# Thirteen of 64 pairs of k rows of the down projections by Strassen's algorithm, columns in two halves

## The chip, the cores and the metric

The kernel runs on one core of one Trainium2 chip, as one program in one launch. The metric is the device time of that launch in microseconds (us). The engines are called as the profile calls them: PE does matrix multiplications, PEld is its weight load, DVE is the vector engine, ACT the scalar engine, POOL the general one, SP issues most of the loads. SBUF is the memory in which the engines work, PSUM the banks into which PE accumulates. A "tile" here is a named piece of one of them.

## The reference, cut to what matters

A trunk of two decoder layers on 256 tokens of width 2048, all in float32. Layer 0 has stick-breaking attention, layer 1 differential attention; each is followed by a squared-ReLU MLP, and each half of a layer ends in a residual with a factor and a layer norm.

```python
D_MODEL = 2048; SEQ = 256; DEPTH = 2; D_FF = 4 * D_MODEL
DEEPNORM_ALPHA = (2 * DEPTH) ** 0.25

def squared_relu_mlp(x, w_up, w_down):
    h = jax.nn.relu(x @ w_up)
    return (h * h) @ w_down

for layer in range(DEPTH):
    ...   # h = attention of this layer
    x = layer_norm(DEEPNORM_ALPHA * x + h, ln_g[layer, 0], ln_b[layer, 0])
    x = layer_norm(DEEPNORM_ALPHA * x + squared_relu_mlp(x, mlp_w_up[layer], mlp_w_down[layer]),
                   ln_g[layer, 1], ln_b[layer, 1])
```

The down projection multiplies h*h, 256 x 8192, by `w_down`, 8192 x 2048, once per layer. It is the place of the change.

## The kernel before

**Three products for one.** PE is given values of a type (float32r) that keeps fewer bits than float32. Each operand is therefore split into a part `hi`, written by ACT as a copy into that type, and a part `lo`, the difference, written by DVE (`split`, L56 to L62). A product is made of three matmuls, hi·hi, hi·lo and lo·hi, all added up in one PSUM bank. So each weight that comes in costs ACT one pass and DVE one pass before PE can use it, and L59 and L62 are the lines of nearly all of their work.

**Weights.** `wchunk` (L67) loads 128 x 1024 values (512 KB) into one of four staging tiles `st` by a load on SP's queue, takes a pair of tiles `wh` and `wl` from a ring of seven (`ring`, L64), and splits. A chunk is one k row block (128 rows of the weight matrix) by 1024 columns, or two row blocks by 512.

**PSUM.** There are eight banks of 128 x 512: five under the tag "acc", three under the tag "at" (`acc`, L53). "at" also serves transposes and attention.

**The stages.** Layer 0: queries, keys, values and attention, output projection, MLP; layer 1 the same with its own attention. An MLP (`mlp`, L264) first runs the up projection: sixteen blocks of 512 hidden columns. The first goes by token rows and is transposed (L269 to L275); the others go by column (`by_column`, L175), so that the hidden values come out with the hidden index on the partitions, and `folded` (L194) and L280 add the two halves of a bank, apply the squared ReLU and write `hT`, sixteen tiles that hold all of h*h in float32. The operand of the up projection is `xT` (L79), the transposed and split input, one tile of 16 k blocks.

The down projection (L286 to L325) keeps the whole result, 2 blocks of 128 tokens (t) by 4 blocks of 512 columns (n), in the eight banks `a`. It goes once over the 64 k blocks of the hidden index. For every two of them a tile `hp` (two buffers) takes the split of h (L306); for each k, two chunks bring the 2048 columns, and PE does 2 x 4 x 3 = 24 matmuls of 128 x 512. The last `lag` = 5 k blocks are held back and done output by output, so that `residual` (L125) and `layernorm` (L133) of the first token block run while PE works on the second. For these last chunks `space` (L291) lends buffers of `hT` that are no longer read. `load_gb` brings the gain and bias of the layer norm into other such buffers.

**Order of work.** The kernel states tiles and operations; waits, and the place of each operation in its engine's list, are worked out when the program is built. The planner goes by the written order, but puts an operation that it reckons to be ready ahead of one that isn't. Each engine then runs its list from front to back. A tile with `bufs=n` under one tag may exist n times at once; a further one waits until the oldest has been read for the last time.

## Time and profile before

| | |
|---|---|
| device time, median of 3 runs | 2219.82 us (2218.59 to 2220.05) |
| the profiled execution's own time | 2220.36 us |
| its span | 2218.5 us |
| PE, DVE, ACT busy, share of the span | 99%, 61%, 46% |
| moved by DMA | 417.81 MB, mean 188 GB/s |
| PE clock granted, mean | 0.999 |
| up stage of layer 0, about | 428 to 762.6 us |
| down stage of layer 0, about | 762.6 to 1113 us |
| up and down stage of layer 1, about | 1527 to 1859.8, 1859.8 to 2208 us |

The profile is one execution. Times in it are counted from the span's start. Groups of instructions are by line, engine, operation and tile (out<-in), with the count, the busy time in us and the mean duration of one in ns, then the idle time of the engine just before them and what ended it. A row of the timeline or of the chain starts with its start time and its length; "x2" means that two instructions were merged into the row. A stage row gives its window, its length, then for PE, PEld, DVE, ACT and POOL the busy time and the number of instructions in it, the granted PE clock as a share, the mean busy share of the DMA engines, and GB/s. A wait row names the engine and line that waited, who ended the wait, and the total, the count and the longest. Matmuls are pipelined, so the durations of neighbours overlap; their pitch is the distance of their starts.

### The profile page before, as it was taken

The numbers are of one execution on the slowest core, as the hardware profiler recorded it, in microseconds if no ns is written. First come the engines' busy times: TensorE is split into PE (matmuls) and PEld (weight loads), VectorE is DVE, ScalarE is ACT, GpSimd is POOL, SyncE is SP. The second block draws the span as 40 slices with busy tenths as digits, with TensorE's granted clock in tenths as the row PEclk, the third lists the DMA queues.
The fourth block names the chain that finished last, engine by engine and source line by source line (L and its number), as shares of the span: only waits on it lengthen the run. The fifth ranks groups of instructions, "written<-read, shape, count | busy, mean of one in ns | idle before, by whom it ended". The sixth has DMA issues, their size and how long they took to land.

```text
span 2218.5 us, 29307 instructions
## 1 busy us (share of the span) xinstructions
PE 2201.0 (99%) x11314; PEld 1870.9 (84%) x11314; DVE 1360.0 (61%) x1865; ACT 1025.4 (46%) x1346; POOL 14.4 (1%) x20
## 2 busy tenths in 40 slices
PE   8999999999999999999999999999999999999998
PEld 7888888888888888888888888888888888888886
DVE  5776665755555554555678787667555555555546
ACT  5655553444444444444445555434444444444442
POOL 0000000000000000000000000000000000000000
PEclk9999999999999999999999999999999999999999
DMA  8555557566666666666565555556666666666663
GB/s 267 175 161 171 164 174 232 162 190 190 190 190 190 193 216 202 194 192 192 169 205 162 180 159 183 194 186 190 190 189 191 189 190 199 221 196 192 192 196 115
DMA packets 177149, 417.81 MB, mean 188 GB/s; under 512 B 13137, under 2 KB 13649, under 8 KB 177010
## 3 DMA queue, kind: packets, MB, share of 16 engines
q1 hardware_dynamic: 171056, 405.52, 60.0%
q10 hardware_dynamic: 5954, 10.42, 1.5%
q8 instruction: 88, 1.44, 0.3%
q14 instruction: 51, 0.42, 0.1%
HBM read 413.80 MB, written 2.10 MB: 187 GB/s over the span
## 4 chain that ended last, share of the span: by engine, by line
PE 98%; DVE 1%; DMA 0%; issue 0%; ACT 0%; SPq 0%; POOL 0%; DVEq 0%; POOLq 0%; ACTq 0%
PE acc L151 83%; PE at L151 14%; PE at L93 1%; DMA st<-in_sb_w_qkv_dram 0%; DVE wl L62 0%; DVE xs L144 0%; DVE xs L143 0%; PE at L518 0%; PE at L491 0%; DVE stats L128 0%; DVE xs L127 0%; DVE xT L62 0%; PE at L274 0%; ACT wh L59 0%; DVE on L511 0%
## 5 line engine op out<-in xcount | busy, mean ns | idle before, releaser
L62 DVE TENSOR_TENSOR wl<-st,wh 128x1024 fp32r<-128x1024 f32 x768 | 938.5, 1224 | 785.9 <-ACT wh L59 771.5
L59 ACT ACTIVATE wh<-st 128x1024 fp32r<-128x1024 f32 x768 | 811.8, 1059 | 1038.0 <-PE acc L151 956.0
L151 PE MATMUL acc<-xT,wh 128*128 128x512 f32 x2944 | 1016.8, 395 | 0.3 <-ACT k L59 0.3
L151 PE MATMUL acc<-xT,wl 128*128 128x256 f32 x2944 | 790.4, 279 | 0.0
L151 PEld LDWEIGHTS acc<-xT,wh 128*128 128x128 f32 x2944 | 541.4, 188 | 113.0 <-ACT k L59 1.0
L151 PEld LDWEIGHTS acc<-xT,wl 128*128 128x128 f32 x2944 | 553.7, 188 | 15.8
L151 PE MATMUL acc<-wh,hp 128*128 128x512 f32 x1280 | 414.3, 390 | 0.0
L151 PEld LDWEIGHTS acc<-wh,hp 128*128 128x128 f32 x1280 | 240.3, 188 | 49.6
L151 PE MATMUL at<-wh,hp 128*128 128x512 f32 x768 | 256.2, 390 | 0.0
L151 PE MATMUL acc<-wl,hp 128*128 128x512 f32 x640 | 249.4, 390 | 0.0
L151 PE MATMUL acc<-wh,xT 128*128 128x512 f32 x640 | 209.4, 396 | 1.2 <-ACT wh L59 1.2
L151 PEld LDWEIGHTS at<-wh,hp 128*128 128x128 f32 x768 | 144.2, 188 | 29.8
L151 PE MATMUL at<-wl,hp 128*128 128x512 f32 x384 | 149.6, 389 | 0.0
L151 PEld LDWEIGHTS acc<-wh,xT 128*128 128x128 f32 x640 | 120.6, 189 | 26.4 <-ACT wh L59 1.6
L151 PEld LDWEIGHTS acc<-wl,hp 128*128 128x128 f32 x640 | 120.2, 188 | 24.9
L151 PE MATMUL acc<-wl,xT 128*128 128x512 f32 x320 | 126.2, 395 | 0.0
L197 ACT ACTIVATE evb<-acc 128x256 f32<-128x256 f32 x184 | 69.2, 377 | 39.6 <-PE acc L151 35.9
L151 PEld LDWEIGHTS at<-wl,hp 128*128 128x128 f32 x384 | 72.1, 188 | 15.0
L151 PE MATMUL acc<-wh,oTa 128*128 128x512 f32 x256 | 80.5, 391 | 0.0
L151 PE MATMUL acc<-wh,oTb 128*128 128x512 f32 x256 | 80.4, 392 | 0.0
L151 PEld LDWEIGHTS acc<-wl,xT 128*128 128x128 f32 x320 | 60.5, 189 | 11.5
L200 DVE TENSOR_TENSOR evs<-acc,evb 128x256 f32<-128x256 f32 x152 | 60.2, 417 | 0.8
(104 smaller groups left out, 1055.4 us busy)
## 6 DMA issues: line engine op xcount, KB each, us to landing
st<-in_mlp_w_up_dram SPq DMA_DIRECT2D x256, 512.0 KB, 3.7
st<-in_mlp_w_down_dram SPq DMA_DIRECT2D x256, 512.0 KB, 4.2
st<-in_sb_w_qkv_dram SPq DMA_DIRECT2D x96, 512.0 KB, 4.0
st<-in_kv_w_dram SPq DMA_DIRECT2D x64, 512.0 KB, 4.3
st<-in_sb_w_o_dram SPq DMA_DIRECT2D x32, 512.0 KB, 3.9
st<-in_diff_w_q_dram SPq DMA_DIRECT2D x32, 512.0 KB, 4.2
st<-in_diff_w_o_dram SPq DMA_DIRECT2D x32, 512.0 KB, 4.5
gb<-in_ln_g_dram ACTq DMA_DIRECT2D x16, 256.0 KB, 5.1
```

The costliest lines, as they stand in the source:

```text
L59: nc.scalar.activation(hi, src, AF.Copy)
L62: nc.vector.tensor_tensor(lo, src, hi.bitcast(F32), op=ALU.subtract)
L93: nc.tensor.transpose(pt[:, i * P:(i + 1) * P], src[:, i * P:(i + 1) * P], ident)
L151: nc.tensor.matmul(o, l, r, start=start, stop=stop)
L197: nc.scalar.activation(b, psum[:, T:], AF.Copy, scale=scale)
L200: nc.vector.tensor_tensor(s, psum[:, :T], b, op=ALU.add)
```

## The change

The 2048 output columns are done in two halves of 1024, one after the other, each over all 64 k blocks. In a half the result takes four banks (`main`, 2 token blocks by 2 column blocks); the other four are free for `side`. Two k blocks by 1024 columns are called a pair here; there are 32 per half, 64 per layer. A pair is a product of 2 x 2 blocks (token block by k block) with 2 x 2 blocks (k block by column block), eight block products, or 24 matmuls. In 13 of the 64, those numbered 3, 7, ... 27 in the first half and 3, 7, ... 23 in the second, `seven` does it with seven block products (Strassen's algorithm in Winograd's form): sums of hidden blocks (`sf`) and of weight blocks (`t13`, `t24`) are made in float32 on DVE, then split like anything else, and three products go straight into `main`, while p1, p5, p6 and p7 collect in the `side` banks over all sevens of a half. After the last of them `share_out` adds the side banks into the residual `xs`, with the factor ALPHA, and `rest` later adds the main banks.

Further edits: `xT` becomes four tiles under one tag with four buffers, which serve `seven` for sums and their splits between the up projection and the next use of xT; h is split twice, once per half; `hp` has three buffers; the rows held back at the end are the last ten of the second half, in chunks of two row blocks by 512 columns, and `space` lends three pairs of buffers, not four.

The diff, without the lines in which `xT[:, k, ...]` becomes `xT[k // 4][:, k % 4, ...]`:

```diff
+SEVEN = ((3, 7, 11, 15, 19, 23, 27), (3, 7, 11, 15, 19, 23))
...
-    xT = base.tile([P, KT, 2, T], F32R, name="xT")
+    def xtile(name="xT", dtype=F32R):
+        return base.tile([P, 4, 2, T], dtype, tag="xT", bufs=4, name=nm(name))
+
+    xT = [xtile() for _ in range(4)]
...
-            a = [[acc("at"), acc("at"), acc("at"), acc()], [acc() for _ in range(4)]]
-            lag = 5
-            spare = [4]
+            lag = 10
+            spare = [3]
...
-            sets = [[k] for k in range(FT - lag)] + [list(range(FT - lag, FT))]
-            hp = {}
-            for ks in sets:
...
+            def hidden(k, tag="hp", bufs=3):
+                h = pool.tile([P, 2, 2, T], F32R, tag=tag, bufs=bufs, name=nm("hp"))
+                split(h[:, 0], h[:, 1], hT[k // 4][:, k % 4:k % 4 + 2, :])
+                return h
+
+            def three(o, x, w, start, stop):
+                mm(o, x[0], w[0], start, False)
+                mm(o, x[0], w[1], False, False)
+                mm(o, x[1], w[0], False, stop)
+
+            def seven(k, n0, main, side, first, end):
+                st = [wp.tile([P, 2, 512], F32, tag="st", bufs=ST_BUFS, name=nm("st")) for _ in range(2)]
+                for kk in range(2):
+                    nc.sync.dma_start(st[kk], down[(k + kk) * P:(k + kk + 1) * P, n0:n0 + CH].rearrange(
+                        "p (a b) -> p a b", a=2))
+                (b11, b12), (b21, b22) = [[s[:, a, :] for a in range(2)] for s in st]
+                tf, sx, tw13, tw24 = [xtile(n, d).rearrange("p a c t -> p (a c t)") for n, d in (
+                    ("tf", F32), ("sp", F32R), ("tw", F32R), ("tw", F32R))]
+                t13, t24 = [tf[:, i * CH:(i + 1) * CH].rearrange("p (a b) -> p a b", a=2) for i in range(2)]
+                sf = pool.tile([P, 4, P], F32, tag="r", bufs=2, name=nm("sf"))
+                sp = sx[:, :CH].rearrange("p (c a b) -> p c a b", c=2, a=4)
+                tw13, tw24 = [(w[:, :CH], w[:, CH:]) for w in (tw13, tw24)]
+                h = hidden(k)
+                hf = hT[k // 4][:, k % 4:k % 4 + 2, :]
+                a11, a21, a12, a22 = [hf[:, i // 2, i % 2 * P:(i % 2 + 1) * P] for i in range(4)]
+                tt = nc.vector.tensor_tensor
+                w11 = ring()
+                split(w11[0][:, :512], w11[1][:, :512], b11)
+                w2 = ring()
+                split(w2[0], w2[1], st[1].rearrange("p a b -> p (a b)"))
+                tt(sf[:, 0, :], a21, a22, op=ALU.add)
+                tt(sf[:, 1, :], sf[:, 0, :], a11, op=ALU.subtract)
+                tt(sf[:, 2, :], a11, a21, op=ALU.subtract)
+                tt(sf[:, 3, :], a12, sf[:, 1, :], op=ALU.subtract)
+                split(sp[:, 0], sp[:, 1], sf)
+                tt(t13[:, 0, :], b12, b11, op=ALU.subtract)
+                tt(t13[:, 1, :], b22, b12, op=ALU.subtract)
+                tt(t24[:, 0, :], b22, t13[:, 0, :], op=ALU.subtract)
+                tt(t24[:, 1, :], b21, t24[:, 0, :], op=ALU.subtract)
+                split(*tw13, tf[:, :CH])
+                split(*tw24, tf[:, CH:])
...
+                p1, p5, p6, p7 = side
+                three(p1, x(0, 0), cols(w11, 0), first, end)
+                three(main[0][0], x(1, 0), cols(w2, 0), False, False)
+                three(main[0][1], xsum(3), cols(w2, 1), False, False)
+                three(p5, xsum(0), cols(tw13, 0), first, end)
+                three(p7, xsum(2), cols(tw13, 1), first, end)
+                three(p6, xsum(1), cols(tw24, 0), first, end)
+                three(main[1][0], x(1, 1), cols(tw24, 1), False, False)
+
+            def share_out(side, nh):
+                p1, p5, p6, p7 = side
+                y = [[xs[:, t, (2 * nh + n) * 512:(2 * nh + n + 1) * 512] for n in range(2)] for t in range(NT)]
+                u, v = [pool.tile([P, 512], F32, tag="r", bufs=2, name=nm("r")) for _ in range(2)]
+                stt, tt = nc.vector.scalar_tensor_tensor, nc.vector.tensor_tensor
+                nc.scalar.activation(u, p1, AF.Copy)
+                stt(y[0][0], y[0][0], ALPHA, p1, op0=ALU.mult, op1=ALU.add)
+                stt(y[0][1], y[0][1], ALPHA, p5, op0=ALU.mult, op1=ALU.add)
+                stt(y[1][1], y[1][1], ALPHA, p5, op0=ALU.mult, op1=ALU.add)
+                tt(u, u, p6, op=ALU.add)
+                tt(v, u, p7, op=ALU.add)
+                tt(y[0][1], y[0][1], u, op=ALU.add)
+                stt(y[1][0], y[1][0], ALPHA, v, op0=ALU.mult, op1=ALU.add)
+                tt(y[1][1], y[1][1], v, op=ALU.add)
+
+            def rest(t, n, psum):
+                y = xs[:, t, n * 512:(n + 1) * 512]
+                nc.vector.tensor_tensor(y, y, psum, op=ALU.add)
+                nc.vector.bn_stats(stats[t][:, n, :], y)
+
+            fast = SEVEN
+            side = [acc() for _ in range(4)]
+            main = [[acc("at"), acc("at")], [acc("at"), acc()]]
+            for nh in range(2):
+                n0 = nh * CH
+                if nh == 1:
+                    main, old = [[acc() for _ in range(2)] for _ in range(NT)], main
+                    for t in range(NT):
+                        for n in range(2):
+                            rest(t, n, old[t][n])
+                    side = [acc("at"), acc("at"), acc("at"), acc()]
+                for j in range(FT // 2 - (lag // 2 if nh else 0)):
+                    k = 2 * j
+                    if nh == 1 and k == FT // 2:
+                        gb = load_gb(layer, 1, gb_of, hT[k // 4][:, 0, 0:1])
+                    if j in fast[nh]:
+                        seven(k, n0, main, side, j == fast[nh][0], j == fast[nh][-1])
+                        if j == fast[nh][-1]:
+                            share_out(side, nh)
+                        continue
+                    h = hidden(k)
+                    for kk in range(2):
+                        wh, wl = wchunk(down[(k + kk) * P:(k + kk + 1) * P, n0:n0 + CH].rearrange(
+                            "(a p) n -> p a n", p=P))
...
+            ks = list(range(FT - lag, FT))
+            hs, chunks = {}, {}
+            for i, k in enumerate(ks[::2]):
+                hs[k] = hidden(k) if i < 3 else hidden(k, "hT", FT // 4)
+            for n in range(2):
+                for k in ks[::2]:
+                    chunks[k, n] = wchunk(down[k * P:(k + 2) * P, n0 + n * 512:n0 + (n + 1) * 512].rearrange(
+                        "(a p) n -> p a n", p=P), space if n == 1 and k >= FT - 6 else ring)
+            if not last:
+                xT[:] = [xtile() for _ in range(4)]
+            for t in range(NT):
+                for n in range(2):
+                    for k in ks:
...
+                    rest(t, 2 + n, main[t][n])
+                layernorm(t, stats[t], gb, last)
```

More of the change, by code (lines that the diff above doesn't have):

```diff
@@ L296, in space @@
                 return [pool.tile([P, CH], F32R, tag="hT", bufs=FT // 4, name=nm(s)) for s in ("wh", "wl")]
-            sets = [[k] for k in range(FT - lag)] + [list(range(FT - lag, FT))]
-            hp = {}
-            for ks in sets:
-                chunks = {}
-                for k in ks:
-                    if k % 2 == 0:
-                        tag, bufs = ("hT", FT // 4) if k == FT - 2 else ("hp", 2)
-                        hp[k // 2] = pool.tile([P, 2, 2, T], F32R, tag=tag, bufs=bufs, name=nm("hp"))
-                        split(hp[k // 2][:, 0], hp[k // 2][:, 1], hT[k // 4][:, k % 4:k % 4 + 2, :])
-                        if k == FT // 2:
-                            gb = load_gb(layer, 1, gb_of, hT[k // 4][:, 0, 0:1])
-                    for nh in range(2):
-                        chunks[k, nh] = wchunk(
-                            down[k * P:(k + 1) * P, nh * CH:(nh + 1) * CH].rearrange("(a p) n -> p a n", p=P),
-                            space if len(ks) > 1 and nh else ring)
-                for t in range(NT):
-                    ts = slice(t * P, (t + 1) * P)
-                    for n in range(4):
-                        ns = slice(n % 2 * 512, (n % 2 + 1) * 512)
-                        for k in ks:
-                            h, (wh, wl) = hp[k // 2], chunks[k, n // 2]
-                            mm(a[t][n], h[:, 0, k % 2, ts], wh[:, 0, ns], k == 0, False)
-                            mm(a[t][n], h[:, 0, k % 2, ts], wl[:, 0, ns], False, False)
-                            mm(a[t][n], h[:, 1, k % 2, ts], wh[:, 0, ns], False, k == FT - 1)
-                        if ks[-1] == FT - 1:
-                            residual(t, n, a[t][n], stats[t])
-                    if ks[-1] == FT - 1:
-                        layernorm(t, stats[t], gb, last)
@@ new lines, in hidden, with x, xsum, cols @@
+            def hidden(k, tag="hp", bufs=3):
[37 more added lines that the diff above has]
+                split(*tw24, tf[:, CH:])
+                def x(kk, t):
+                    return [h[:, c, kk, t * P:(t + 1) * P] for c in range(2)]
+                def xsum(i):
+                    return [sp[:, c, i, :] for c in range(2)]
+                def cols(w, a):
+                    return [p[:, a * 512:(a + 1) * 512] for p in w]
+                p1, p5, p6, p7 = side
[6 more added lines that the diff above has]
+                three(main[1][0], x(1, 1), cols(tw24, 1), False, False)
@@ new lines, in rest @@
+            def rest(t, n, psum):
[28 more added lines that the diff above has]
+                            for n in range(2):
+                                ns = slice(n * 512, (n + 1) * 512)
+                                three(main[t][n], [h[:, c, kk, t * P:(t + 1) * P] for c in range(2)],
+                                      (wh[:, 0, ns], wl[:, 0, ns]), k + kk == 0, nh == 0 and k + kk == FT - 1)
@@ L328, in trunk @@
+            for t in range(NT):
+                for n in range(2):
+                    for k in ks:
+                        h, (wh, wl) = hs[k - k % 2], chunks[k - k % 2, n]
+                        three(main[t][n], [h[:, c, k % 2, t * P:(t + 1) * P] for c in range(2)],
+                              (wh[:, k % 2, :], wl[:, k % 2, :]), False, k == FT - 1)
+                    rest(t, 2 + n, main[t][n])
+                layernorm(t, stats[t], gb, last)
     with tc.tile_pool(name="sb", bufs=1) as pool:
```

18 lines of the change are left out of this document (9 added, 9 removed).

## The prediction

> **What bounds the kernel now.** First the page's engine shares and the chain that ended last, then the two down stages in the stage table (time, engine busy times, clock, DMA).
>
> ```profile
> span 2218.5 us, 29307 instructions
> PE 2201.0 (99%) x11314; PEld 1870.9 (84%) x11314; DVE 1360.0 (61%) x1865; ACT 1025.4 (46%) x1346; POOL 14.4 (1%) x20
> PE 98%; DVE 1%; DMA 0%; issue 0%; ACT 0%; SPq 0%; POOL 0%; DVEq 0%; POOLq 0%; ACTq 0%
> ...
> 762.60:1111.00 348.40, 348.39 (x1545) 288.39 (x1544) 188.52 (x197) 152.47 (x163) 0.92 (x1) 1.00 0.62 193
> 1859.80:2208.00 348.20, 348.20 (x1537) 288.25 (x1536) 185.13 (x192) 145.29 (x154) 0.92 (x1) 1.00 0.60 189
> ```
>
> The chain lies on PE for 98% of the span. In the down stages PE has no gap at all, at full clock (1.00), while DVE works 188.5 of 348.4 us, ACT 152.5, the DMA engines 62%. A matmul taken away there shortens the kernel by its whole pitch, as long as what the change gives DVE still fits behind PE. The pitch stands in the chain in order of time; one k row of weights shows as 15 matmuls on "acc" banks, with 9 on "at" banks between the rows:
>
> ```profile
> 764.79 3.40 PE acc L151 x15
> 770.23 3.40 PE acc L151 x15
> ...
> 1080.31 3.40 PE acc L151 x15
> ```
>
> From the first to the last are 58 k rows: (1080.31 − 764.79) / 58 = 5.44 us, so 5.44 / 24 = 0.2267 us for each 128x512 matmul, from the first row to the last (3.40 / 15 agrees). 1536 of them make 348.2 us, the length of a down stage.
>
> What waits for whom, over the whole span, says how far ahead of PE the weights are prepared:
>
> ```profile
> ACT wh L59 <- PE acc L151: 956.0, 564, 15.4
> PEld acc L151 <- DVE xT L62: 0.9, 2, 0.4
> PEld acc L151 <- ACT xT L59: 0.8, 3, 0.3
> ```
>
> ACT spends 956 us waiting until PE gives back one of the seven pairs of weight buffers; the waits of PE on prepared data are under 1 us each. Preparation is ahead by the whole ring.
>
> **What is removed.** A pair of k rows by half the columns (a "pair" below) takes 2 k × 2 token blocks × 2 column blocks × 3 = 24 matmuls, 5.44 us. `seven` issues 7 × 3 = 21, 4.76 us. 13 pairs per layer, 2 layers: 78 matmuls fewer, all 128x512 with 128x128 weights as before: 78 × 0.2267 = **−17.68 us**. The bytes read stay: two 512 KB loads per pair.
>
> **What is added on DVE.** Groups by line and shape; the first three rows are from the first down stage alone, the others from the whole span:
>
> ```profile
> L62 DVE TENSOR_TENSOR wl<-st,wh 128x1024 fp32r<-128x1024 f32 x119 | 145.6, 1226 | 151.6 <-ACT wh L59 146.6
> L59 ACT ACTIVATE wh<-st 128x1024 fp32r<-128x1024 f32 x119 | 125.7, 1057 | 166.6 <-PE acc L151 164.8 <-DMA st<-in_mlp_w_down_dram 1.6
> L62 DVE TENSOR_TENSOR hp<-hT,hp 128x512 fp32r<-128x512 f32 x29 | 19.9, 684 | 0.0
> ...
> L59 ACT ACTIVATE hp<-hT 128x512 fp32r<-128x512 f32 x64 | 40.3, 632 | 15.8 <-PE acc L151 15.7
> L127 DVE SCALAR_TENSOR_TENSOR xs<-xs,acc 128x512 f32<-128x512 f32 x26 | 17.4, 683 | 17.9 <-PE acc L151 17.9
> L128 DVE BATCH_NORM_STATS2 stats<-xs 128x6 f32<-128x512 f32 x32 | 21.6, 690 | 0.5
> L143 DVE SCALAR_TENSOR_TENSOR xs<-xs,mv,gb 128x512 f32<-128x512 f32 x32 | 22.7, 746 | 0.0
> L485 DVE SCALAR_TENSOR_TENSOR e<-e,rs,e 128x128 f32<-128x128 f32 x8 | 2.8, 346 | 0.0
> ```
>
> An ordinary pair costs DVE one hp split and two wl splits: 0.684 + 2 × 1.226 = 3.14 us under 5.44 of PE. A seven costs seven ops on 128x512 (hp, w11, sp, four weight sums), three on 128x1024 (w2, tw13, tw24) and four on 128x128 (the hidden sums): 7 × 0.684 + 3 × 1.226 + 4 × 0.346 = 9.85 us, against 4.76 of PE. The sevens stand every fourth pair, so the balance is over four: DVE 9.85 + 3 × 3.14 = 19.26 us, PE 4.76 + 3 × 5.44 = 21.08. DVE fits at 91%, by full durations. Overlap between neighbours takes some off:
>
> ```profile
> 2169.86 2.36 DVE L62 TENSOR_TENSOR wl<-st,wh 128x1024 fp32r<-128x1024 f32 x2 [1.34 <-ACT wh L59]
> ```
>
> Two splits back to back take 2.36, not 2 × 1.226 = 2.45, so some 0.09 per op; over 14 + 9 ops 2.1 us: 17.2, or 81%, is the lower bound. ACT: five more 512-wide or wider passes per seven, 3 × 0.632 + 3 × 1.057 = 5.07 us, with three ordinary pairs of 2.75 us 13.3 of 21.08.
>
> Balance over four pairs is worth nothing without lookahead. Call 0 the time at which PE leaves one seven. The ring holds seven chunks, so by then the three ordinary pairs behind it (16.32 us of PE) can be split already, and the slot for the next w11 is free; w2's comes free 2.72 later, the xT buffers of tf, sp and tw at 0, the hp slot (now three) at 5.44, when the first of the three pairs is done. DVE's 9.85 us can thus be over at 10 to 12, and PE wants them at 16.32: 4 us of slack. Taken as 0; what it costs if the cover is gone is the first rival. The two staging buffers that a seven holds during its sums leave two for the next chunks, and a load lands in 4.2 us against 5.44 per two chunks:
>
> ```profile
> st<-in_mlp_w_down_dram SPq DMA_DIRECT2D x256, 512.0 KB, 4.2
> ```
>
> The second pass over hT repeats 32 hp splits per layer (counted above, one per pair). `share_out` adds 8 DVE ops twice per layer, 8 × 0.683 = 5.5 us, and `rest` does at the half's seam 4 × (0.683 + 0.690) = 5.5 us of what used to be at the end.
>
> **What is moved, and queues.** After the last seven of a half `share_out` waits for p6, and at the seam `rest` waits for the first half's last matmuls; both stand in the code ahead of the next chunks on DVE. Whether those queue behind depends on the order of DVE's list. The same situation exists at the end of the up projections, where `folded` and hT of the last block wait for PE (L200, L280), in the timeline (DVE's rows, and PE's first down matmul):
>
> ```profile
> 761.11 1.22 DVE L62 TENSOR_TENSOR wl<-st,wh 128x1024 fp32r<-128x1024 f32 x1 [1.55 <-ACT wh L59]
> 762.25 0.75 DVE L200 TENSOR_TENSOR evs<-acc,evb 128x256 f32<-128x256 f32 x2
> 762.59 0.39 PE L151 MATMUL at<-wh,hp 128*128 128x512 f32 x1
> 762.91 0.75 DVE L280 SCALAR_TENSOR_TENSOR hT<-evs 128x256 f32<-128x256 f32 x2
> 763.58 0.42 DVE L200 TENSOR_TENSOR evs<-acc,evb 128x256 f32<-128x256 f32 x1
> 764.22 1.23 DVE L62 TENSOR_TENSOR wl<-st,wh 128x1024 fp32r<-128x1024 f32 x1 [0.22 <-ACT wh L59]
> 765.36 0.42 DVE L280 SCALAR_TENSOR_TENSOR hT<-evs 128x256 f32<-128x256 f32 x1
> 765.70 0.42 DVE L200 TENSOR_TENSOR evs<-acc,evb 128x256 f32<-128x256 f32 x1
> ```
>
> A down chunk's split (764.22) was put between the last blocks' ops, though it is written after all of them: the build's planner lets a later op go ahead of one that isn't ready. PE's own list does it too:
>
> ```profile
> 428.47 0.60 PE L274 MATMUL at<-cst,r 128*128 128x128 f32 x4
> 428.82 0.48 PE L151 MATMUL acc<-xT,wh 128*128 128x512 f32 x1
> 429.32 0.66 PE L274 MATMUL at<-cst,r 128*128 128x128 f32 x4
> ```
>
> A matmul of the next block stands between transposes that are written ahead of it. So the seams are costed near nothing, with three places that can show:
>
> - Start of down: `side` is allocated first and takes four acc banks, so main[1][1] gets the one freed last, at the last evs (765.70 + 0.42 = 766.12 above). PE begins down at 762.59 and would want it after 9 matmuls, at 764.6 (before, a[1][3] was wanted after 21, at 767.4). Cost 0 if PE's list is rearranged, 1.5 us if not; times two layers 0 to 3.0. I take 1.0, near the end that the PE rows support.
> - Tail (last ten k rows of the second half): the third hidden pair needs the hp slot that PE releases only at the tail's start; PE wants it after 12 matmuls, 2.72 us, and it takes 0.632 + 0.684 and up to one 1.226 op in the way, 1.3 to 2.5 plus two handovers: 0 to 1.0 per layer, 0 to 2.0 in all, taken as 0.6. Ring and spare hT buffers hold the ten weight chunks, as before.
> - xT becomes four tiles: at most the 0.9 + 0.8 us of the two PEld waits above could go; taken as 0, −1.7 kept for the range.
>
> The end stays as it is, since the last matmul is still followed by one add, one bn_stats and the layer norm:
>
> ```profile
> 2207.78 0.39 PE L151 MATMUL acc<-wh,hp 128*128 128x512 f32 x1
> 2208.21 0.69 DVE L127 SCALAR_TENSOR_TENSOR xs<-xs,acc 128x512 f32<-128x512 f32 x1 [1.98 <-PE acc L151]
> ...
> 2214.00 1.41 DVE L144 SCALAR_TENSOR_TENSOR xs<-xs,rstd,gb 128x512 f32<-128x512 f32 x2
> ```
>
> **Sum.** −17.68 + 1.0 + 0.6 = −16.1 us. The profiled execution took 2220.36 us, its span 2218.5 and 1.9 around it; it stands 0.54 above the median of 2219.82. 2220.36 − 16.1 = 2204.3, less 0.54: **2203.7 us**. Its own range is −17.68 − 1.7 to −17.68 + 5.0, or 2200.4 to 2207.1.
>
> **Rivals.**
>
> 1. DVE becomes the bound, and the kernel slower. Inside a seven, sp, tw13 and tw24 each go DVE, ACT, DVE; if DVE idles through each ACT pass for want of ready work, 0.632 + 2 × 1.057 = 2.75 us are added: 19.26 + 2.75 = 22.0 over four pairs, 0.93 above PE's 21.08. With 26 sevens that is 24 us: −16.1 + 24 = +8, 2228. Below 21.08 it costs nothing; the break-even is at 16.1 / 26 = 0.62 above, 21.7 us; halfway, a loss of 8 us, 2212. For: the sum of DVE in a down stage, 51 × 3.14 + 13 × 9.85 + 4 × 5.5 + 16 × 0.746 for the layer norms = 322 of PE's 1497 × 0.2267 = 339 us, and the 146.6 us for which DVE waited on ACT in the first down stage. Against: those waits end with ACT's own wait for PE (164.8), they are surplus; the planner fills gaps with other chunks; overlap brings the sum down. Chance of the slower part 0.10, of the halfway part 0.08.
>
> 2. DVE's list keeps the written order at `share_out` and `rest`. After p6's end DVE still has 5 ops (3.4 us), then an hp and a wl split (1.9), while PE has only 0.68 of matmuls left and one more that needs no wl: 4.4 us of PE idle, twice a layer; at the seam rest starts 2 us ahead of the end, so 5.5 + 1.9 − 2.0 − 0.2 = 5.2. 14 us a layer, 28 in all: −16.1 + 28 = +12, 2232. Against: the rows at 764.22 and 428.82. [...] Chance 0.04.
>
> 3. PE's pace is set by the weight loads, not by the streaming.
>
> ```profile
> L151 PEld LDWEIGHTS acc<-wh,hp 128*128 128x128 f32 x1280 | 240.3, 188 | 49.6
> ```
>
> Then a matmul taken away is worth a load, 0.188 us: 78 × 0.188 = 14.7 us, and the time is 2203.7 + 3.0 = 2206.7. Against: a pitch of 0.2267 at every one of 58 k rows, with the loads idle in between. Chance 0.03. [...]
>
> That the sevens don't happen at all isn't open: the code issues 21 matmuls for them in every case.
>
> **How the numbers follow.** Forecast 0.75, rival 1 in two parts 0.08 and 0.10, rival 2 0.04, rival 3 0.03. Range: from 2200.4 up to 2213, which takes in the forecast's own range, rival 1 halfway and rival 3 (by the page too), and leaves out some 0.16 plus the forecast's edges. A measurement of this kernel tells 0.2%, 4.4 us, from no change. Faster by more: the forecast, rival 3 and the larger part of rival 1 halfway, 0.83. Slower by more: rival 2 and most of rival 1, 0.12. Between: 0.05.
>
> **What would show it.** Right: PE's matmul count 78 lower; each down stage some 340 us with PE without gaps, stages before unchanged to 1 us; DVE 80 to 95% busy there; ACT still waiting for PE more than for anything else. Rival 1: PE gaps just ahead of each seven, ended by DVE writing tw or sp, DVE at 100%. Rival 2: gaps of some 4 us at two places per layer, after the last seven of a half, and 5 at the seam, with `share_out` and `rest` ahead of wl on DVE. Rival 3: pitch in the sevens off 0.2267. The start-of-down cost: a gap of up to 1.5 us after the ninth down matmul, ended by the last evs. A loss elsewhere, by a planner that orders the whole program otherwise, would make the prediction wrong in a way that no step here covers.

## The result, and the profile after

| | before | after |
|---|---|---|
| device time, median | 2219.94 us (2218.59 to 2220.71, 4 runs) | 2203.70 us (2202.27 to 2204.24, 4 runs) |
| ratio, with its 95% interval | | 0.9926 [0.9909, 0.9944] |
| the profiled execution's own time, its span | 2220.36, 2218.5 us | 2204.09, 2202.3 us |

The change makes the kernel 16.2 us faster, and the time is the predicted one. In the kernel after, the lines have moved: the split is L60 (ACT) and L63 (DVE), the matmul L155, the transposes L97, the hidden sums of a seven L336 to L339, its weight sums L341 to L344, `share_out` L373 to L380, `rest` L384 and L385, the layer norm L139 to L148.

The page of after, the lines that answer to those of before: span, instructions by engine, shares of the chain.

```profile
span 2202.3 us, 29620 instructions
PE 2182.8 (99%) x11236; PEld 1854.9 (84%) x11236; DVE 1560.0 (71%) x2247; ACT 1116.0 (51%) x1492; POOL 14.4 (1%) x20
PE 97%; DVE 1%; DMA 1%; ACT 0%; issue 0%; SPq 0%; POOL 0%; DVEq 0%; ACTq 0%
```

PE has 78 matmuls fewer (11314 to 11236) and is 18.2 us less busy; DVE has 200 us more and is still not the engine on which the chain lies. The stage table of after: the two down stages (the first from its first matmul to the first one behind it; the second from 0.15 us ahead of its first matmul, which starts at 1852.45, to just behind the start of its last, 2191.55), and two groups of four pairs (one seven and three ordinary pairs) in the first of them. Columns as before: window, length, busy time and instructions of PE, PEld, DVE, ACT, POOL, clock, DMA share, GB/s.

```profile
763.39:1104.87 341.48, 341.47 (x1514) 282.50 (x1513) 287.09 (x376) 195.91 (x233) 0.92 (x1) 1.00 0.61 198
1852.30:2191.80 339.50, 339.50 (x1499) 280.89 (x1497) 280.18 (x367) 188.88 (x225) 0.92 (x1) 1.00 0.60 194
824.08:845.16 21.08, 21.08 (x95) 17.45 (x94) 17.88 (x24) 12.70 (x16) 0.00 (x0) 1.00 0.60 198
845.16:866.24 21.08, 21.08 (x95) 17.45 (x94) 16.98 (x20) 12.69 (x16) 0.00 (x0) 1.00 0.63 199
```

PE has no gap in either stage, at full clock. A group takes 21.08 us, 93 matmuls of 0.2267, and DVE is busy 17.9 or 17.0 of it. The two rows differ by four operations (x24, x20): the hidden sums are made some sevens ahead, one set lies in the first of these groups and none in the second. So a group with a set of hidden sums costs DVE 17.9. The first stage with the transposes that lie in it took 350.34 us before (762.59 to 1112.93), so it lost 8.86 us. The second took 347.94 from its first matmul to its last before (1859.84 to 2207.78) and 339.10 after (1852.45 to 2191.55), so it lost 8.84; 39 matmuls by the pitch are 8.84.

The wait table of after over the whole span, the rows with which ACT, then DVE, then PE waited (total, count, longest):

```profile
ACT wh L60 <- PE acc L155: 685.8, 464, 10.3
ACT wh L60 <- DMA st<-in_mlp_w_down_dram: 20.5, 21, 4.1
...
PE at L97 <- DVE xs L148: 1.0, 1, 1.0
```

ACT still waits for PE above all else, 685.8 us where it was 956.0: preparation is ahead of PE, with less to spare. The last row is new in size: PE's transposes wait 1.0 us for the layer norm.

What the operations of a seven cost on DVE, in the groups by form of after, and one hidden sum in its timeline (start, duration):

```profile
L63 DVE TENSOR_TENSOR tw<-tf,tw 128x1024 fp32r<-128x1024 f32 x52 | 63.6, 1223 | 0.0
L341 DVE TENSOR_TENSOR tf<-st 128x512 f32<-128x512 f32 x26 | 17.8, 686 | 2.2 <-DMA st<-in_mlp_w_down_dram 2.2
...
774.33 0.29 DVE L336 TENSOR_TENSOR sf<-hT 128x128 f32<-128x128 f32 x1
```

They cost what the rows of before said, 1.22 and 0.69 (with 0.68 for the splits of 512); the hidden sums are shorter than the 0.346 taken from another operation of that size. With 0.29 for these and 0.09 of overlap per operation, a seven is 7 × 0.685 + 3 × 1.224 + 4 × 0.29 − 14 × 0.09 = 8.37 us, an ordinary pair 3.14 − 0.27 = 2.87, and a group 8.37 + 3 × 2.87 = 16.98. That it equals the second row above is chance, since this group has no hidden sums in it; the row to compare with is 17.88, so the overlap was not 0.09 but some 0.05 per operation. By this sum an ordinary pair leaves DVE 5.44 − 2.87 = 2.57 us to spare, and a seven takes 8.37 − 4.76 = 3.6 us more than PE gives it. These two numbers return in the experiments; they are estimates, on the low side for DVE's work, by 0.9 us per group.

**The three places where the prediction had put seams.** First the start of down. The timeline of after, PE's first and tenth down matmul, and on DVE the last evs:

```profile
763.39 0.39 PE L155 MATMUL at<-wh,hp 128*128 128x512 f32 x1
764.91 0.75 DVE L204 TENSOR_TENSOR evs<-acc,evb 128x256 f32<-128x256 f32 x2
765.44 0.39 PE L155 MATMUL acc<-wh,hp 128*128 128x512 f32 x1
```

The tenth matmul, the first on an "acc" bank, comes 2.05 us after the first, nine times 0.2267: no gap. The last evs are done 2.3 us after PE's first down matmul, where it had been 3.5 before (766.12 less 762.59), and the bank that main[1][1] took was free in time. It can't have been the last one freed, as the prediction had it, for its first matmul starts 0.2 us before the last evs are done (764.91 + 0.75 = 765.66). The term of 1.0 us was 0.

Then `share_out` of the first half, DVE's rows in the timeline of after:

```profile
911.01 0.68 DVE L376 TENSOR_TENSOR r<-r,acc 128x512 f32<-128x512 f32 x1
911.61 1.22 DVE L63 TENSOR_TENSOR wl<-st,wh 128x1024 fp32r<-128x1024 f32 x1
912.74 0.68 DVE L377 TENSOR_TENSOR r<-r,acc 128x512 f32<-128x512 f32 x1
```

A later chunk's split stands between two operations of `share_out`: the planner did there what it had done at the end of the up projections. The tail of the second half has no gap either (339.50 us busy of 339.50 in the second stage), so the term of 0.6 us was 0 too.

### The profile page after: what moved, and what is told of

Its sections match the earlier page's. It is cut to its first block, busy times and chain, and to the rows that moved or that the text cites. A ratio compares the mean times of both kernels' runs of the same rounds, so it can differ in the third digit from the quotient of the medians.

```text
span 2202.3 us, 29620 instructions
## 1 busy us (share of the span) xinstructions
PE 2182.8 (99%) x11236; PEld 1854.9 (84%) x11236; DVE 1560.0 (71%) x2247; ACT 1116.0 (51%) x1492; POOL 14.4 (1%) x20
## 4 chain that ended last, share of the span: by engine, by line
PE 97%; DVE 1%; DMA 1%; ACT 0%; issue 0%; SPq 0%; POOL 0%; DVEq 0%; ACTq 0%
PE acc L155 83%; PE at L155 14%; PE at L97 1%; DMA st<-in_sb_w_qkv_dram 0%; DVE wl L63 0%; DMA st<-in_kv_w_dram 0%; DVE xs L148 0%; DVE xs L147 0%; ACT wh L60 0%; PE at L626 0%; PE at L599 0%; DVE xT L63 0%; PE at L278 0%; DVE stats L385 0%; DVE xs L384 0%
## 5 line engine op out<-in xcount | busy, mean ns | idle before, releaser
L63 DVE TENSOR_TENSOR wl<-st,wh 128x1024 fp32r<-128x1024 f32 (+1 forms) x768 | 919.4, 1204 | 518.7 <-ACT wh L60 513.4
L60 ACT ACTIVATE wh<-st 128x1024 fp32r<-128x1024 f32 (+1 forms) x768 | 796.3, 1043 | 786.1 <-PE acc L155 685.8
L155 PE MATMUL acc<-xT,wh 128*128 128x512 f32 x2944 | 1016.1, 395 | 0.3 <-ACT k L60 0.3
L155 PE MATMUL acc<-xT,wl 128*128 128x256 f32 x2944 | 789.3, 278 | 0.0
L155 PEld LDWEIGHTS acc<-xT,wh 128*128 128x128 f32 x2944 | 540.2, 188 | 112.9 <-ACT k L60 1.2
L155 PEld LDWEIGHTS acc<-xT,wl 128*128 128x128 f32 x2944 | 553.3, 188 | 15.9
L155 PE MATMUL acc<-wh,hp 128*128 128x512 f32 x1084 | 354.1, 389 | 0.0
L155 PEld LDWEIGHTS acc<-wh,hp 128*128 128x128 f32 x1084 | 203.4, 188 | 42.1
L155 PE MATMUL at<-wh,hp 128*128 128x512 f32 x652 | 221.2, 389 | 0.0
L155 PE MATMUL acc<-wl,hp 128*128 128x512 f32 x542 | 210.9, 389 | 0.0
L155 PE MATMUL acc<-wh,xT 128*128 128x512 f32 x640 | 209.0, 395 | 1.7 <-ACT wh L60 1.6
L60 ACT ACTIVATE hp<-hT 128x512 fp32r<-128x512 f32 x128 | 80.3, 631 | 133.5 <-PE acc L155 110.5
L155 PEld LDWEIGHTS at<-wh,hp 128*128 128x128 f32 x652 | 122.4, 188 | 25.3
L155 PEld LDWEIGHTS acc<-wh,xT 128*128 128x128 f32 x640 | 120.4, 189 | 26.9 <-ACT wh L60 2.0
L155 PE MATMUL at<-wl,hp 128*128 128x512 f32 x326 | 126.8, 389 | 0.0
L155 PE MATMUL acc<-wl,xT 128*128 128x512 f32 x320 | 126.1, 394 | 0.3 <-DVE wl L63 0.3
L155 PEld LDWEIGHTS acc<-wl,hp 128*128 128x128 f32 x542 | 101.7, 188 | 21.2
L63 DVE TENSOR_TENSOR hp<-hT,hp 128x512 fp32r<-128x512 f32 x128 | 87.9, 688 | 43.2 <-ACT hp L60 43.2
L155 PE MATMUL acc<-wh,oTa 128*128 128x512 f32 x256 | 80.5, 390 | 0.0
L155 PE MATMUL acc<-wh,oTb 128*128 128x512 f32 x256 | 80.4, 391 | 0.0
L155 PEld LDWEIGHTS at<-wl,hp 128*128 128x128 f32 x326 | 61.2, 188 | 12.8
```

The lines of the kernel that those rows point to most:

```text
L60: nc.scalar.activation(hi, src, AF.Copy)
L63: nc.vector.tensor_tensor(lo, src, hi.bitcast(F32), op=ALU.subtract)
L155: nc.tensor.matmul(o, l, r, start=start, stop=stop)
```

## The experiments

The kernel before ran beside each of them on the same chip. Where an experiment changes one line of the kernel after, the diff is against that.

### The form alone: halves without sevens

```diff
-SEVEN = ((3, 7, 11, 15, 19, 23, 27), (3, 7, 11, 15, 19, 23))
+SEVEN = ((), ())
...
-                nc.vector.tensor_tensor(y, y, psum, op=ALU.add)
+                nc.vector.scalar_tensor_tensor(y, y, ALPHA, psum, op0=ALU.mult, op1=ALU.add)
...
-            side = [acc() for _ in range(4)]
...
-                    side = [acc("at"), acc("at"), acc("at"), acc()]
```

> The form of the change (two halves, h split twice, four xT tiles, ten rows held back) without any seven; all 64 pairs are ordinary, rest takes the factor ALPHA. Theory (the whole gain is the 78 matmuls, at 0.2267 us each): 17.7 us come back, and what the form itself costs stays: 2219.9 to 2221.4 us, PE without gaps in the down stages, which take 348.2 us each again. Rival (part of the gain comes from the form, by shorter seams): under 2217 us.

Measured: 2220.68 us (2219.39 to 2222.32) against 2219.71, ratio 1.0004 [0.9995, 1.0013]. From its page and its waits:

```profile
PE 2200.0 (99%) x11314; PEld 1868.8 (84%) x11314; DVE 1408.5 (63%) x1929; ACT 1059.8 (48%) x1410; POOL 14.4 (1%) x20
PE at L97 <- DVE xs L148: 1.0, 1, 1.0
```

With the sevens gone and everything else of the form kept (two halves, h split twice, `rest` at the half's seam, ten rows held back), the gain is gone. So it lies in the 78 matmuls, and the form costs 1 us by the medians (−1 to 3 by the interval); the wait for the layer norm belongs to the form and not to the sevens.

### Where the sevens stand: seven in a row

```diff
-SEVEN = ((3, 7, 11, 15, 19, 23, 27), (3, 7, 11, 15, 19, 23))
+SEVEN = (tuple(range(3, 10)), tuple(range(3, 9)))
```

> The same 13 sevens per layer, but next to each other (pairs 3 to 9 of the first half, 3 to 8 of the second). All totals stay as in the changed kernel. Theory (the three ordinary pairs between two sevens hide DVE's work): in a row DVE needs 8.6 us per seven where PE needs 4.76, so 3.8 us of gap for each after a lead of some 8 us per half; 19 + 15 us per layer, 68 in all: 2272 us, from 2255 to 2300 since there is only one set of buffers for sums, and the gaps end with DVE writing tw or sp. Rival (only the totals of DVE and PE over a stage count): 2204 us.

Measured: 2280.27 us (2278.01 to 2282.14), ratio 1.0272 [1.0256, 1.0287]. The same 11236 matmuls and 2247 DVE operations now take 76.6 us more than in the kernel after. The first seven of them in the stage table of this kernel and a stretch behind those of the second half, one of the gaps in its timeline, and the wait that names their releaser:

```profile
763.20:831.00 67.80, 56.64 (x228) 40.87 (x227) 62.30 (x98) 38.49 (x50) 0.00 (x0) 1.00 0.39 121
1000.00:1040.00 40.00, 35.30 (x139) 27.38 (x138) 32.16 (x43) 20.76 (x25) 0.00 (x0) 0.91 0.60 198
800.10 0.73 PE L155 MATMUL acc<-tw,sp 128*128 128x512 f32 x2 [0.97 <-ACT tw L60]
PE acc L155 <- ACT tw L60: 15.8, 20, 1.5
```

PE idles 11.2 of 67.8 us, nearly always just ahead of a product that needs a seven's sums (two gaps, 1.6 us, lie ahead of one with plain weights), while DVE is busy 62.3 of them. What ends most gaps is ACT's copy of the sums, not DVE's split, as the expectation and the first rival had it. Over both down stages the matmuls start 63 us late at full clock, near the 68 of the theory, and 10 us more where the clock fell to 0.50, which the theory left out. That is the first rival's picture, brought about by place alone: these sums are free where ordinary pairs lie between the sevens, and not where none do.

### DVE's list in the written order

The DVE work of the three ordinary pairs behind `share_out`, and behind `rest`, is placed after these in DVE's list; nothing waits that did not have to, only the order of the list is different.

```diff
+                            behind, left = rest(t, n, old[t][n]), 3
...
+                            behind, left = share_out(side, nh), 3
...
+                    left -= 1
+                    order = tc.issue_after(getattr(behind, 'ins', behind)) if left >= 0 else nullcontext()
+                    with order:
+                        h = hidden(k)
+                        two = [wchunk(down[(k + kk) * P:(k + kk + 1) * P, n0:n0 + CH].rearrange(
+                            "(a p) n -> p a n", p=P)) for kk in range(2)]
```

> The changed kernel, with the DVE work of the three pairs that follow share_out and of the three that follow rest at the seam put behind these in DVE's list (order alone, no new wait). Theory (the planner's list, which puts ready splits ahead of share_out and rest, is what makes these places free): 4.4 us of PE idle after each share_out and 5.2 at each seam, 14 per layer, 28 in all: 2232 us, between 2224 and 2236. Rival (the lead of the ring covers these places in any order): 2204 us.

Measured: 2237.27 us (2234.64 to 2239.15), ratio 1.0074 [1.0058, 1.0091]: 33.6 us above the kernel after, where 28 had been worked out. DVE and PE in the timeline of this kernel around the first `share_out`:

```profile
912.56 0.69 DVE L380 TENSOR_TENSOR xs<-xs,r 128x512 f32<-128x512 f32 x1
913.16 0.68 DVE L63 TENSOR_TENSOR hp<-hT,hp 128x512 fp32r<-128x512 f32 x1
913.76 2.35 DVE L63 TENSOR_TENSOR wl<-st,wh 128x1024 fp32r<-128x1024 f32 x2
...
915.03 0.80 PE L155 MATMUL at<-wl,hp 128*128 128x512 f32 x1 [3.46 <-DVE wl L63]
...
916.48 0.63 PE L155 MATMUL at<-wh,hp 128*128 128x512 f32 x1
916.91 0.63 PE L155 MATMUL at<-wl,hp 128*128 128x512 f32 x1
```

The last operation of `share_out`, an hp split, a wl split, and only then PE goes on, after 3.46 us: rival 2 as it was written. The waits of PE on wl, and the stage table of this kernel around that gap and behind the last of its kind:

```profile
PE acc L155 <- DVE wl L63: 14.6, 4, 3.8
PE at L155 <- DVE wl L63: 6.9, 2, 3.5
```

```profile
911.50:915.00 3.50, 0.07 (x1) 0.00 (x0) 3.50 (x6) 0.00 (x0) 0.00 (x0) 0.82 0.00 0
915.00:919.00 4.00, 3.97 (x9) 3.14 (x10) 4.00 (x5) 0.31 (x1) 0.00 (x0) 0.50 0.62 184
919.00:925.00 6.00, 6.00 (x25) 4.87 (x24) 4.31 (x9) 3.62 (x5) 0.00 (x0) 0.87 0.85 315
...
2181.62:2188.00 6.38, 6.38 (x28) 5.29 (x29) 5.79 (x6) 1.06 (x1) 0.00 (x0) 1.00 0.67 210
```

Six gaps, 21.5 us in all, some 3.6 each: shorter than worked out. A matmul's row is 0.39 us long where the pitch is 0.2267, so a gap delays PE by 0.16 more than its row says; for six that makes 22.5. Behind the first gap the granted clock is 0.50 up to 920.5 (0.87 on average from 919 to 925), and there the pitch is 916.91 − 916.48 = 0.43 instead of 0.2267. The clock falls behind four more of the gaps, for 3.4 or 6.8 us each time, 23.9 us in all, and that costs 10 us; behind the last gap, which ends at 2181.62, it stays at 1.00. The profile of this kernel is 35 us longer than that of the kernel after, and what 22.5 + 10 leave of it are shorter waits of PE for hp (1.3 and 0.6 us).

So the length of a single gap does not decide it: the last of these gaps, 3.46 us, is followed by no fall, and with the sum made seven times (below) the clock falls to 0.50 although no gap of the down stages is longer than 1.3 us.

### More sevens: every third pair, every second pair

```diff
-SEVEN = ((3, 7, 11, 15, 19, 23, 27), (3, 7, 11, 15, 19, 23))
+SEVEN = (tuple(range(2, 30, 3)), tuple(range(2, 24, 3)))
```

> A seven at every third pair instead of every fourth: 10 and 8 per layer, 18 instead of 13. Theory (PE is the bound as long as DVE's work with its overlaps fits): DVE per three pairs is 8.59 + 2 x 2.87 = 14.3 us under 15.64 of PE, so another 30 matmuls x 0.2267 = 6.8 us go: 2196.9 us, no gaps of PE in down. Rival (full durations count, DVE becomes the bound): 9.85 + 2 x 3.14 = 16.13 against 15.64, 0.49 us too much in each of 36 groups, 17.6 us lost: 2214 us.

Measured: 2206.27 us (2204.32 to 2208.45), ratio 0.9939 [0.9924, 0.9954], halfway between the two. The stage table of this kernel: a group of three pairs in the first half, then the whole of the first half and of the second up to the held back rows; and pieces of its chain in the second half (start, duration, what):

```profile
822.48:838.12 15.64, 15.64 (x70) 12.95 (x70) 14.81 (x20) 10.16 (x13) 0.00 (x0) 1.00 0.64 207
...
765.00:924.00 159.00, 159.00 (x703) 131.68 (x702) 145.95 (x194) 100.61 (x120) 0.00 (x0) 1.00 0.62 199
924.00:1080.00 156.00, 153.65 (x674) 125.60 (x673) 143.69 (x204) 95.88 (x116) 0.00 (x0) 1.00 0.66 212
```

```profile
934.71 1.15 DVE wl L63
935.88 3.58 DMA st<-in_mlp_w_down_dram
939.47 1.06 ACT wh L60
941.79 4.77 DMA st<-in_mlp_w_down_dram
```

One in three fits: in the first half DVE works 14.8 of every 15.64 us and PE has no gap. The loss begins after the half's seam. From there the chain runs in a loop: a split ends and frees a staging tile, the load into it takes 3.6 to 6.8 us, ACT copies it, DVE splits it. Here the seven of pair 29, `share_out`, `rest` and the seven of pair 2 stand with only four ordinary pairs (30, 31, 0, 1) between the sevens: 4 × 2.57 = 10.3 us to spare against some 11 for the two bursts.

```diff
-SEVEN = ((3, 7, 11, 15, 19, 23, 27), (3, 7, 11, 15, 19, 23))
+SEVEN = (tuple(range(3, 30, 2)), tuple(range(3, 26, 2)))
```

> A seven at every second pair: 14 and 12 per layer, 26 instead of 13. Theory (DVE becomes the bound where its work with overlaps is over PE's): per two pairs DVE needs 8.59 + 2.87 = 11.46 us, PE 10.2; over a layer's down stage 26 x 8.59 + 38 x 2.87 + 22 = 354 us of DVE against 1458 x 0.2267 = 330.5 of PE, so the stage takes 354 to 370 us instead of 339.4: 2233 to 2265 us, slower than before, with gaps of PE that end with DVE or with loads held up by DVE. Rival (PE stays the bound): 156 matmuls fewer than before, 2185 us.

Measured: 2315.36 us (2314.07 to 2319.5), ratio 1.0428 [1.041, 1.0445]: slower, as the theory has it, but by 50 us more than its upper end. A stretch of the first half in this kernel's stage table, a piece of its chain, and ACT's wait for loads of w_down:

```profile
870.00:900.00 30.00, 27.67 (x110) 21.22 (x109) 26.79 (x41) 17.49 (x22) 0.00 (x0) 0.94 0.51 163
...
796.93 0.61 DVE tf L344
797.56 6.73 DMA st<-in_mlp_w_down_dram
...
ACT wh L60 <- DMA st<-in_mlp_w_down_dram: 206.7, 163, 7.5
```

DVE is not even full, 26.8 of 30 us. ACT waits 206.7 us for loads, ten times the 20.5 of the kernel after, although the DMA engines move less per second (163 GB/s) than there (198). So it is not bandwidth: on the chain the load starts as one of DVE's weight sums ends, when DVE has given a staging tile back. Adding up DVE's busy time prices none of that, nor the clock of 0.94 behind the gaps.

### More DVE work in the same sevens

```diff
-                tt(t13[:, 0, :], b12, b11, op=ALU.subtract)
+                for _ in range(7):
+                    tt(t13[:, 0, :], b12, b11, op=ALU.subtract)
```

> The changed kernel with the first weight sum of each seven made seven times over (six more DVE passes of 128x512, same values). Theory (back to back they cost 0.60 us each): 16.98 measured + 3.6 = 20.6 of 21.08 us per four pairs, DVE still fits in steady groups, but has only 0.5 us per group to catch up after share_out and rest: 2204 to 2214 us. Rival (full durations count, DVE is late by 19.26 + 4.1 - 21.08 = 2.3 us in each of 26 groups): 60 us, 2264 us.

Measured: 2221.77 us (2218.73 to 2225.87), ratio 1.0012 [1.0003, 1.0022], some 8 us above the upper end. A group of four pairs in the first half (one with hidden sums, to be set against 17.88 above and not 16.98), a stretch behind the seam, and two neighbouring pieces of it in this kernel's stage table; then ACT's wait:

```profile
824.20:845.30 21.10, 21.10 (x95) 17.48 (x94) 20.93 (x30) 12.62 (x15) 0.00 (x0) 1.00 0.63 197
922.50:1080.00 157.50, 155.19 (x675) 127.36 (x675) 147.39 (x204) 88.12 (x105) 0.00 (x0) 0.99 0.63 204
992.97:996.38 3.41, 1.70 (x6) 0.87 (x6) 3.16 (x4) 3.32 (x5) 0.00 (x0) 1.00 0.83 288
996.38:999.79 3.41, 3.41 (x9) 2.66 (x9) 3.41 (x5) 1.92 (x4) 0.00 (x0) 0.50 0.72 208
...
ACT wh L60 <- DMA st<-in_mlp_w_down_dram: 99.3, 89, 5.2
```

Up to the seam DVE is busy 20.9 of each 21.1 us and PE has no gap: the balance over four pairs holds almost to the last tenth of a microsecond. All gaps of the down stages lie behind the seam, in both layers, with late loads again. And no gap of the down stages is longer than 1.3 us, yet the clock falls: PE was busy half of the 3.41 us ahead of 996.38, and the next 3.41 us ran at 0.50. A steady group that fits is not enough; the seam needs a reserve of its own.

### Which part of the seam: two spacings of sixteen

Sixteen sevens per layer, three more than in the kernel after; once with the last seven of the first half early and the first of the second late, once with the first half dense and the second spaced by four.

```diff
-SEVEN = ((3, 7, 11, 15, 19, 23, 27), (3, 7, 11, 15, 19, 23))
+SEVEN = (tuple(range(2, 27, 3)), tuple(range(5, 24, 3)))
```

> A seven at every third pair, but none near the seam: pairs 2 to 26 of the first half (9), 5 to 23 of the second (7), 16 per layer. Theory (the run with 18 lost its gain because share_out, rest and a seven met at the seam and the 0.9 us that DVE has left per three pairs never made that up): without that 3 x 3 x 2 = 18 more matmuls than in the changed kernel go, x 0.2267 = 4.1 us: 2199.6 us, without gaps of PE. Rival (the second half can't hold one seven in three at all): gaps in the second half, 2204 us or more.

```diff
-SEVEN = ((3, 7, 11, 15, 19, 23, 27), (3, 7, 11, 15, 19, 23))
+SEVEN = (tuple(range(2, 30, 3)), tuple(range(3, 24, 4)))
```

> A seven at every third pair in the first half (2 to 29, 10 of them), at every fourth in the second (3 to 23, 6), so also 16 per layer, but close to the seam. Theory (the seam is where DVE falls behind; at one seven in four it has 4.1 us per group to make up): a few gaps after the seam, then none: 2200 to 2204 us. Rival (the second half is what doesn't hold one in three; the seam does no harm): 2199.6 us.

Measured: 2198.78 us (2198.06 to 2200.02), ratio 0.9905 [0.989, 0.992], and 2199.31 us (2198.67 to 2200.12), ratio 0.9907 [0.9892, 0.9922]. Both reach the sum of their matmuls. The first shows that a second half with one in three is no trouble in itself, which the rival had thought. The second has its last seven at 29 as the kernel with every third pair has, and only five ordinary pairs up to the next one, and still no loss; the few gaps that the theory expected after the seam are absent. Its time is the 2199.6 of its rival, but the first of the two runs speaks against that rival's reason. So neither half is at fault alone. What fits all of these runs is a balance on DVE's time at the seam, made afterwards: the ordinary pairs between the two sevens by 2.57 us, less 11 for `share_out` and `rest`, less 3.6 for the next seven (7.2 where its first sum is made seven times, six more at 0.6 each); and then what each later group wins back (the group's length less its DVE time, by the rows with hidden sums).

| spacing | ordinary pairs at the seam | balance there, us | won back per group, us | loss seen behind the seam |
|---|---|---|---|---|
| kernel after | 7 | +3.4 | 3.2 | none |
| every third pair | 4 | −4.3 | 0.8 | yes |
| sum made seven times | 7 | −0.2 | 0.2 | yes |
| seam left free | 10 | +11 | 0.8 | none |
| dense, then by four | 5 | −1.7 | 3.2 | none |

With an overlap of 0.05 per operation, as the row of 17.88 has it, each balance would be an estimated 1 to 2 us lower; the signs stay. A balance below zero shows as a loss where the groups behind it win little back. This is argued from sums, not shown by a single wait; the next run is the only one that was predicted from it. ACT's wait for loads of w_down goes with the loss, too: 75.8 us with every third pair and 99.3 with the sum made seven times, but 14.7 and 13.9 in these two kernels of sixteen.

### Seventeen sevens, and the kernel after again

```diff
-SEVEN = ((3, 7, 11, 15, 19, 23, 27), (3, 7, 11, 15, 19, 23))
+SEVEN = (tuple(range(2, 30, 3)), tuple(range(6, 25, 3)))
```

> One more seven than in the best so far: pairs 2 to 29, every third, in the first half (10), and 6 to 24, every third, in the second (7), 17 per layer. Theory (after the seam DVE needs 11 us of spare time before the next seven, and each ordinary pair gives 5.44 - 2.87 = 2.57 us): here 8 ordinary pairs stand between the two, 20.6 us, where the run with 18 had 4, 10.3 us; so no gaps, and 24 matmuls fewer than in the changed kernel, x 0.2267 = 5.4 us: 2198.3 us, 1.4 us below the kernels with 16. Rival (one in three in both halves is too much whatever the seam): 2204 us or more, with gaps in the second half.

> The changed kernel once more, on the same chip and with more rounds, to compare the one with 17 with it. Every theory: 2203.7 us, ratio to the kernel before 0.9926.

Measured: seventeen 2198.32 us (2196.81 to 2199.39), ratio 0.9903 [0.9888, 0.9918]; the kernel after, on the same chip, 2203.40 us (2201.99 to 2203.59), ratio 0.9924 [0.9911, 0.9936]. From the stage table of the kernel with seventeen, the first down stage without its ends:

```profile
765.00:1080.00 315.00, 315.00 (x1391) 260.85 (x1390) 288.04 (x389) 194.67 (x233) 0.00 (x0) 1.00 0.65 208
```

PE has no gap with DVE at 91%. Eight ordinary pairs between the sevens of pairs 29 and 6 give 20.6 us at the seam, a balance of +6.0. The medians differ by 5.1 us in favour of seventeen; the intervals of the two ratios overlap a little, so this advantage over the kernel after is likely rather than certain, and the one over the kernel before is certain.

## Why the prediction was right, step by step

**The matmul term** (−17.68) held: 8.86 and 8.84 us in the two down stages are −17.7. It is worth the pitch, not a weight load: a group of 93 matmuls takes 21.08 us, where rival 3 would have it 3 × (0.2267 − 0.188) = 0.12 longer. For the second price of rival 3 that the prediction's range takes in, no run shows a figure; what the runs show is 17.70 / 78 = 0.227 us per matmul. Halves without sevens give the whole of it back.

**DVE's balance** held between its bounds: 17.9 us per four pairs, where 17.2 (with overlap) to 19.26 (full durations) had been worked out. The price of the hidden sums was off, 0.29 and not 0.346, and the overlap took away 1.2 us and not 2.1. The break-even of rival 1 over four pairs is borne out as far as 20.9 us, by the run that has this much and no gap in its first half; no run here lies between that and PE's 21.08.

**The lookahead** is what makes the sums free: with the same operations in a row, 76.6 us are lost. The 4 us of slack were a rough sum, yet on the safe side, since 3.6 us more DVE work per seven still fits in steady groups.

**The planner** made `share_out` and `rest` free, as the rows at 764.22 and 428.82 of before suggested; in the written order they cost 33.6 us. Rival 2's 28 us for that order come within 6 of this, in part by luck: its gaps were too long (28 us in all, where the rows show 21.5), and the halved clock, 10 us, was not in it. It was wrong about which order is built.

**Wrong: the two small terms.** The prediction set +1.0 for main[1][1] at the start of down and +0.6 for the hp slot in the tail. Both measured 0. The span still came out 16.2 us shorter, and not 17.6, for two reasons that no step named. The first down matmul starts 0.8 us later than before (763.39 against 762.59). This delay is there by PE's 501st matmul (100.92 against 100.06), long ahead of the first operation of a seven (a hidden sum at 458.0). The first weights already arrived later: ACT's first wh copy of the query weights in the timeline of before, then of after:

```profile
10.30 1.06 ACT L59 ACTIVATE wh<-st 128x1024 fp32r<-128x1024 f32 x1 [1.62 <-DMA st<-in_sb_w_qkv_dram]
```

```profile
10.83 1.06 ACT L60 ACTIVATE wh<-st 128x1024 fp32r<-128x1024 f32 x1 [2.27 <-DMA st<-in_sb_w_qkv_dram]
```

In the second profile of the kernel after, the first down matmul starts at 761.2, and the span is 2200.2; in the experiments, whose edits all lie in the down stages, it starts between 761.1 and 763.3. So these 0.8 us, either way, belong to the execution and not to the change: from the first down matmul on, the two profiles of the kernel after are 17.0 and 16.9 us shorter than that of before. The other part lies between the layers: from the end of one down stage to the start of the next 747.6 us pass (1104.87 to 1852.45), 746.9 before (1112.93 to 1859.84). There the layer norm is late. DVE's rows of after, and PE's first transpose behind them:

```profile
1108.49 0.26 DVE L139 BATCH_NORM_AGGREGATE mv<-stats 128x2 f32<-128x24 f32 x1
1109.87 1.23 DVE L63 TENSOR_TENSOR wl<-st,wh 128x1024 fp32r<-128x1024 f32 x1 [1.13 <-ACT wh L60]
1111.01 0.15 DVE L141 TENSOR_SCALAR ve<-mv 128x1 f32<-128x1 f32 x1
...
1113.29 0.63 PE L97 MATMUL at<-cst,xs 128*128 128x128 f32 x4 [1.00 <-DVE xs L148]
```

A chunk's split that has to wait 1.13 us for ACT stands in DVE's list ahead of the layer norm's second operation. That operation's input is written by 1108.75 (1108.49 + 0.26), and it starts at 1111.01, behind the split, as the list has it; PE waits 1.0 us at the end of it, 0.2 before. So the ledger by rows is +0.8 − 8.86 + 0.67 − 8.84 = −16.2. That the forecast of 2203.7 was met to the decimal is partly luck: 1.6 us had been allowed for, in places where nothing was lost, and 1.5 turned up in others, 0.8 of them by the execution alone.

**Wrong in size: the price of rival 1.** It took what DVE has too much per group, times the number of groups. Every second pair shows what that leaves out: some 95 us slower than before, where the expectation by this price ended 45 above it. There DVE gave staging tiles back late, the loads started late, ACT waited 206.7 us for them (20.5 in the kernel after), and the clock fell where gaps lay close together (0.94 on average from 870 to 900). A halfway case such as the 2212 of the prediction is therefore narrow; the same kernel with 3.6 us more DVE work per seven, whose steady groups fit, already lost all of the gain.

What stays open: how the lateness at the seam builds up, operation by operation. The table of balances fits five spacings, but no wait shows it, and the loss comes late: by the count of matmuls the seam lies at 929.8 with every third pair and at 930.4 with the sum made seven times, and PE's first late start comes 62 and 42 us behind it (991.4 and 972.3). What the down stages with every third pair took over their matmuls can be accounted for: they lasted 341.9 us, 2.1 of transposes in it, and 340.4, against 1482 × 0.2267 = 336.0 each, 8.2 us too long. Late starts of PE's matmuls make 8.1 of it; 5.1 show as idle time, and the rest is hidden under the row of the matmul before.

## What to carry to other kernels

Taking matmuls from PE and giving DVE more work paid the full pitch of each matmul here (0.2267 us for each of 78), where the added work was spread so that preparation's lead covered it, and lost 76.6 us where it wasn't: check the balance over the repeating group, and then separately at each seam where other work of DVE comes in a burst. A deadline that was missed cost more than its own length here: with every second pair, where buffers came back late, ACT waited 206.7 us for loads and the time was 50 us above the upper end that had been worked out from DVE's busy time, and in four runs PE's clock fell to 0.50 for 3.4 or 6.8 us at a time behind idle time. And what an added operation costs was decided here by the list that is built for its engine, 33.6 us by the order alone: look there, in the timeline, before an idle time is blamed on the chip.

## What the runs showed of the hardware

**The clock after idle time.** In four runs here PE's clock falls to 0.50 within the down stages (the sevens in a row, the written order, every second pair, the sum made seven times), 22 times in all, each time for 3.4 or 6.8 us, with a pitch of 0.43. It need not be one long gap: with the sum made seven times no gap of the down stages is longer than 1.3 us, and PE was busy for 1.70 of the 3.41 us ahead of the fall at 996.38. Nor does idle time of that size always bring a fall: in the first sevens in a row PE was busy for 1.3 of the 3.41 us from 824.22 on, with gaps of 1.50 and 0.60 us, and the last gap of the written order is 3.46 us long; behind both the clock stayed at 1.00. What decides it is not shown.

**Late loads.** With every second pair the median load of w_down takes 4.8 us from issue to landing, and single ones stand on the chain with 6.7, while the DMA engines are busy 51% and move 163 GB/s. In the first profile of the kernel after the median is 3.9, in its second 4.2, and it is 4.5 with sixteen and seventeen sevens, where PE has no gap. So most of the difference is no sign of lateness, and that a load takes longer where they are less dense is not shown; what goes with the losses is ACT's wait for loads, 206.7 us with every second pair against 14 to 28 in the kernels with sevens but without gaps.
